# A hybrid decoder trunk on one Trainium2 core: adaLN dot products over 2048 columns at once, in two buffers of 2048 columns instead of three of 1024

## The chip, the cores and the metric

One core of one Trainium2 chip runs the whole program. The metric is the device time of one execution in microseconds (us); lower is better. The median of three runs of the kernel before is 2453.43 us (2445.65 to 2476.61).

## What is computed

Two layers of a decoder on 256 tokens of width 2048, all in float32. Each layer begins from a modulation that depends on one conditioning vector `c`; what follows is a token mixer with four head groups and a feed-forward network (FFN) with a short convolution:

```python
cond = silu(c)                                   # (1, 2048)
for l in range(2):
    mod = cond @ ada_w[l] + ada_b[l]             # ada_w[l]: 2048 x 12288
    sh1, sc1, g1, sh2, sc2, g2 = split(mod, 6)   # six vectors of 2048
    h = rms_norm(x, norm_mix[l]) * (1 + sc1) + sh1
    x = x + g1 * hybrid_mixer(h, ...)
    h = rms_norm(x, norm_ffn[l]) * (1 + sc2) + sh2
    x = x + g2 * conv_glu_ffn(h, ...)
```

The matrix `ada_w` is 100 MB a layer, a third of all that is read from HBM for both layers. Only the product of one row vector with it is needed.

## The kernel before

**Layout and stages.** Activations stand transposed: 128 channels on the partitions, the 256 tokens on the free axis, 16 channel chunks. Weights come from HBM in chunks of 128 x 1024 (512 KB) into a ring of four buffers, `raw`. ScalarE (ACT) rounds a chunk to `hi` (line 247), VectorE (DVE) subtracts to get `lo` (line 249), and TensorE (PE) multiplies with both (lines 279, 300, 304, 415). `hi` and `lo` have three buffers each. Stages run one after the other: layer 0's first stage (to about 160 us), its mixer (to 510), its FFN (to 1280), then the same for layer 1. In the FFN `up(g)` runs 22 times over 8 weight chunks each; the matrices of `down` follow in two parts, after g = 11 and after g = 21.

**The adaLN dots.** A product with `ada_w` is done on DVE, not on PE. There are 192 dots: 2 layers x 6 vectors (s = 0 to 5) x 16 channel chunks. A dot takes, for 128 output channels, 2048 columns of `ada_w`. They come in two halves of 128 x 1024, each with its own DMA (512 KB, `ada_load`, line 160) and its own multiply with `cond` that sums along the row (`ada_mul`, line 166, the `scalar_tensor_tensor` of line 167; its sum is fetched by a second small instruction, DVE_READ_ACCUMULATOR). The halves share a ring of three buffers of 1024 columns, the tag `adaw`. After four dots of a vector `ada_sum` (line 180) adds the two sums and the bias, for four chunks at once (lines 183 and 184).

**Who sets their order.** In layer 0's first stage (`mix_in_behind`, line 451) the dots of s = 1 and s = 0 for chunk k stand in line before the weight chunks of k: 32 dots, `ada_dot` at line 172. All others (160) are jobs of `ada_jobs` (line 187): `load_w` calls `tick`, which gives out jobs by a rate per weight chunk, and `mod` (line 225) forces those that are still missing when their vector is needed. A job loads its dot; its multiply is put behind the `lo` of that weight chunk. They get a low priority, and the scheduler that lays down the engines' queues places them among the rest. All DMAs are issued in order by the SP queue. A load of `adaw` waits there until its buffer's last multiply is done, and whatever stands behind it, the next weight chunk included, waits too. On DVE a multiply waits for its load, and the `lo` behind it waits too.

**Other places touched.** `nku` and `cT` (lines 821 and 967) are two small buffers of the sparse attention. `g` (line 1166) is the ring for the FFN's activations, 14 buffers, of which `down` needs 12 at once while one more is written. `Y_ORDER` and the names RATE, ADA_LATE, GATE are unchanged. An FFN begins with `norm_chunk` for 16 chunks (line 391), each with `t` (line 394), an ACT instruction (398) and an `act` (399); for the chunks c to c + 3 it needs the vectors s = 4 and s = 3 of these chunks.

## Time and profile before

| what | value |
|---|---|
| median of three runs | 2453.43 us |
| the profiled execution, its own time | 2452.41 us |
| its span (first to last instruction) | 2450.6 us |
| TensorE's mean granted clock | 0.987 of full |
| busy: PE / DVE / ACT | 2369.3 / 1937.6 / 1225.8 us |
| read from HBM | 603 MB, 248 GB/s over the span |

The profile is of one execution. A group of rows joins instructions of one line, engine and shape: its busy time, the mean of one, and the engine's idle time just before them with what ended it. Busy time of PE covers pipelined matmuls, so a busy PE is not yet one at its peak; how many matmuls it does in a stretch says more. The 1.8 us between span and time lie outside the first and last instruction.

### The profile page before, as it was taken

Reading aid. Unit: us, or ns where it says so; the run is one execution under the profiler, and the core shown is the slowest. Engines: PE = TensorE matmul, PEld = TensorE weight load, DVE = VectorE, ACT = ScalarE, POOL = GpSimd, SP = SyncE. Lnnn points to the kernel's source line nnn. Section 1 sums busy time; section 2 is a strip of 40 time slices with the busy share of each in tenths; the row PEclk is TensorE's granted clock in tenths of the full one; section 3 lists DMA queues with packets and bytes.
Section 4 is the critical chain, followed back from the end, with each engine's and each line's share of the span. In section 5 each row is a group of like instructions: output and inputs, shape, how many; then the busy total and the mean of one; then the engine's idle time right before and its main releaser. Section 6 shows DMA issues by size and latency. Waiting matters only on the chain.

```text
span 2450.6 us, 38162 instructions
## 1 busy us (share of the span) xinstructions
PE 2369.3 (97%) x14496; PEld 2100.5 (86%) x14496; DVE 1937.6 (79%) x3212; ACT 1225.8 (50%) x1880; POOL 25.2 (1%) x40
## 2 busy tenths in 40 slices
PE   7788999989999999999999999999999999999999
PEld 5666999978888888888879999998888888888887
DVE  6679988888888887888876999888887765566755
ACT  2124666446555534556335476554655553355543
POOL 0000000000000000000001000000000000000000
PEclk9999999999999999999999999999999999999999
DMA  9975787987777898778885567898667655556654
GB/s 326 328 275 183 246 270 270 336 290 255 256 255 248 297 320 293 260 240 270 288 295 168 187 218 244 269 321 317 236 231 241 224 191 191 189 186 196 190 190 164
DMA packets 169098, 609.82 MB, mean 249 GB/s; under 512 B 19025, under 2 KB 20945, under 8 KB 168401
## 3 DMA queue, kind: packets, MB, share of 16 engines
q1 hardware_dynamic: 168914, 607.39, 73.0%
q8 instruction: 113, 1.85, 0.3%
q14 instruction: 71, 0.58, 0.1%
HBM read 603.12 MB, written 4.19 MB: 248 GB/s over the span
## 4 chain that ended last, share of the span: by engine, by line
PE 84%; DMA 6%; DVE 6%; ACT 3%; issue 1%; SPq 0%; DVEq 0%; ACTq 0%
PE gt L300 39%; PE gt L304 20%; PE gt L279 9%; DMA adaw<-in_ada_dram 6%; PE gt L415 3%; PE pn L322 3%; DVE adaw L167 2%; PE po L591 1%; DVE lo L249 1%; PE pv L322 1%; PE pq L322 1%; PE s L565 1%; PE tp L586 1%; PE ss L382 1%; ACT hi L247 1%
## 5 line engine op out<-in xcount | busy, mean ns | idle before, releaser
L247 ACT CAST hi<-raw 128x1024 fp32r<-128x1024 f32 (+3 forms) x716 | 741.9, 1037 | 852.9 <-PE gt L300 602.2
L249 DVE TENSOR_TENSOR lo<-raw,hi 128x1024 fp32r<-128x1024 f32 (+3 forms) x716 | 859.7, 1204 | 358.0 <-ACT hi L247 356.3
L300 PE MATMUL gt<-act,hi 128*128 128x512 f32 x2816 | 983.7, 395 | 10.8 <-DVE act L399 7.8
L304 PE MATMUL gt<-act,lo 128*128 128x256 f32 x2816 | 786.6, 280 | 4.0 <-DVE lo L249 4.0
L300 PEld LDWEIGHTS gt<-act,hi 128*128 128x128 f32 x2816 | 530.9, 189 | 133.0 <-DVE act L399 8.6
L304 PEld LDWEIGHTS gt<-act,lo 128*128 128x128 f32 x2816 | 533.4, 190 | 5.3 <-DVE lo L249 5.3
L167 DVE SCALAR_TENSOR_TENSOR adaw<-adaw,cond 128x1024 f32<-128x1024 f32 x384 | 465.3, 1220 | 69.9 <-DMA adaw<-in_ada_dram 68.6
L300 PE MATMUL gt<-g,hi 128*128 128x512 f32 x1408 | 490.5, 394 | 0.2 <-DVE x L1179 0.2
L304 PE MATMUL gt<-g,lo 128*128 128x256 f32 x1408 | 393.0, 279 | 0.0
L300 PEld LDWEIGHTS gt<-g,hi 128*128 128x128 f32 x1408 | 264.4, 188 | 60.3 <-issue 0.4
L279 PE MATMUL gt<-act,hi 128*128 128x256 f32 x1600 | 303.2, 287 | 0.0
L304 PEld LDWEIGHTS gt<-g,lo 128*128 128x128 f32 x1408 | 265.7, 189 | 0.3
L279 PEld LDWEIGHTS gt<-act,hi 128*128 128x128 f32 x1600 | 251.4, 191 | 1.4
L279 PE MATMUL gt<-act,lo 128*128 128x256 f32 x800 | 230.7, 288 | 1.5 <-DVE lo L249 1.5
L279 PEld LDWEIGHTS gt<-act,lo 128*128 128x128 f32 x800 | 153.1, 191 | 2.5 <-DVE lo L249 2.3
L415 PE MATMUL gt<-actw,raw 128*128 128x256 f32 x416 | 105.7, 417 | 26.7 <-ACT actw L396 26.7
L415 PEld LDWEIGHTS gt<-actw,raw 128*128 128x128 f32 x416 | 86.1, 210 | 46.1 <-ACT actw L396 32.6
L1155 ACT ACTIVATE u<-v,vec 128x256 f32<-128x256 f32 x176 | 96.7, 597 | 10.2 <-DVE v L1152 5.3
L621 DVE SCALAR_TENSOR_TENSOR acc<-ug,vec,acc 128x256 f32<-128x256 f32 x240 | 99.1, 478 | 0.0
L1156 DVE SCALAR_TENSOR_TENSOR u<-v,vec,u 128x255 f32<-128x255 f32 x176 | 80.1, 479 | 11.9 <-ACT u L1155 11.9
L1151 ACT COPY v<-gt 128x256 f32<-128x256 f32 x176 | 63.5, 369 | 47.5 <-PE gt L304 34.2
L1159 DVE SCALAR_TENSOR_TENSOR u<-v,vec,u 128x254 f32<-128x254 f32 x176 | 80.1, 479 | 2.6
(290 smaller groups left out, 2152.6 us busy)
## 6 DMA issues: line engine op xcount, KB each, us to landing
adaw<-in_ada_dram SPq DMA_DIRECT2D x384, 512.0 KB, 5.5
raw<-in_wup_dram SPq DMA_DIRECT2D x352, 512.0 KB, 4.3
raw<-in_wdn_dram SPq DMA_DIRECT2D x176, 512.0 KB, 4.4
raw<-in_wo_dram SPq DMA_DIRECT2D x64, 512.0 KB, 5.2
raw<-in_wconv_dram SPq DMA_DIRECT2D x32, 512.0 KB, 4.3
raw<-in_wsqk_dram SPq DMA_DIRECT2D x32, 512.0 KB, 4.3
raw<-in_wlq_dram SPq DMA_DIRECT2D x32, 448.0 KB, 4.8
raw<-in_wnkv_dram SPq DMA_DIRECT2D x32, 412.0 KB, 3.4
```

Source lines behind the costliest of these rows:

```text
L167: nc.vector.scalar_tensor_tensor(w, w, 1.0, cond[:, hf * 1024:hf * 1024 + 1024], op0=ALU.mult, op1=ALU.mult, accum_out=raw[:, hf, j:j + 1],)
L247: nc.scalar.copy(hi[:, :n], raw[:, :n])
L249: sub = nc.vector.tensor_sub(lo[:, :n], raw[:, :n], hi[:, :n].bitcast(F32))
L279: nc.tensor.matmul(ps[m // 2][:, m % 2, :], ww[:, c], x, start=(k == 0 and i == 0 and m % 2 == 0), stop=(k == K - 1 and i == len(prods) - ...
L300: nc.tensor.matmul(banks[m].rearrange("p a t -> p (a t)"), hi[:, c], x2, start=(k == 0), stop=False, skip_group_check=True,)
L304: nc.tensor.matmul(banks[m][:, 1, :], lo[:, c], acts[k][:, 0, :], start=False, stop=(k == K - 1), skip_group_check=True,)
L322: nc.tensor.matmul(o, x[:, tt * P:(tt + 1) * P], ww[:, kk * N + c0:kk * N + c1], start=(k == 0 and i == 0 and first), stop=(k == K - 1 and ...
L415: nc.tensor.matmul(ps[m // 2][:, m % 2, :], ww[:, m * P:(m + 1) * P], xx, start=(first and i == 0 and m % 2 == 0), stop=(last and i == len ...
L621: nc.vector.scalar_tensor_tensor(acc[:, c, :], ug[:, c, j:j + T], w, acc[:, c, :], op0=ALU.mult, op1=ALU.add)
L1155: nc.scalar.activation(u[:, q, :], v, AF.Identity, scale=w2, bias=fb[:, i:i + 1])
L1156: nc.vector.scalar_tensor_tensor(u[:, q, 1:], v[:, :T - 1], w1, u[:, q, 1:], op0=ALU.mult, op1=ALU.add)
L1159: nc.vector.scalar_tensor_tensor(u[:, q, 2:], v[:, :T - 2], w0, u[:, q, 2:], op0=ALU.mult, op1=ALU.add)
```

## The change

The buffer of a dot now holds all 2048 columns, there are two of them, and its two DMAs of 512 KB are issued one after the other into its halves. The 160 dots of `ada_jobs` are one multiply over 2048 columns with one sum; `ada_sum` becomes one addition. The 32 dots of layer 0's first stage keep two multiplies of 1024 columns. To make room, `nku` and `cT` move into the ring `nsq` and `g` has 13 buffers.

```diff
-    def ada_load(l, s, j, hf):
-        w = ap_.tile([P, D // 2], F32, tag="adaw", name="adaw", bufs=3)
+    def ada_load(l, s, j):
+        w = ap_.tile([P, D], F32, tag="adaw", name="adaw", bufs=2)
         with tc.issue_after(last_load[0].ins) if gate[0] else ExitStack():
-            nc.sync.dma_start(w, io["ada"][l, s * KD + j, hf])
+            for hf in range(2):
+                nc.sync.dma_start(w[:, hf * 1024:hf * 1024 + 1024], io["ada"][l, s * KD + j, hf])
         return w
-    def ada_mul(w, s, j, hf, raw):
-        nc.vector.scalar_tensor_tensor(
-            w, w, 1.0, cond[:, hf * 1024:hf * 1024 + 1024], op0=ALU.mult, op1=ALU.mult,
-            accum_out=raw[:, hf, j:j + 1],
-        )
+    def ada_mul(w, out, c):
+        nc.vector.scalar_tensor_tensor(w[:, c], w[:, c], 1.0, cond[:, c], op0=ALU.mult, op1=ALU.mult, accum_out=out)
     def ada_dot(l, s, j, raw):
+        w = ada_load(l, s, j)
         for hf in range(2):
-            ada_mul(ada_load(l, s, j, hf), s, j, hf, raw)
+            ada_mul(w, raw[:, hf, j:j + 1], slice(hf * 1024, hf * 1024 + 1024))
...
-        nc.vector.tensor_add(m[:, c], raw[:, 0, c], raw[:, 1, c])
-        nc.vector.tensor_add(m[:, c], m[:, c], vec(l, "ada_b")[:, s * KD + j - 3:s * KD + j + 1])
+        nc.vector.tensor_add(mods[l, s][:, c], raw[:, c], vec(l, "ada_b")[:, s * KD + j - 3:s * KD + j + 1])
...
-                        for hf in range(2):
-                            dots.append(partial(ada_mul, ada_load(l, s, j, hf), s, j, hf, raw[s]))
+                        dots.append(partial(ada_mul, ada_load(l, s, j), raw[s][:, j:j + 1], slice(0, D)))
...
-            u = mp.tile([P, 3, 2, 64], F32, tag="nku", name="nku", bufs=1)
+            u = mp.tile([P, 512], F32, tag="nsq", name="nku")[:, 0:384].rearrange("p (b g d) -> p b g d", b=3, g=2)
...
-            cT = mp.tile([P, T], F32, tag="cT", name="cT", bufs=1)
+            cT = mp.tile([P, 2, T], F32, tag="nsq", name="cT")[:, 0, :]
...
-                y_ = fp.tile([P, 2, 2, T], F32R, tag="g", name="g", bufs=14)
+                y_ = fp.tile([P, 2, 2, T], F32R, tag="g", name="g", bufs=13)
```

SP's queue in layer 0's first stage, before; each `adaw` is one half, and a wait that names DVE is the one for a free buffer:

```order
L163 DMA adaw_244<-in_ada_dram 128x1024 [waits DMAHW2_49,DVE_49]
L163 DMA adaw_247<-in_ada_dram 128x1024 [waits DMAHW3_49,DVE_49]
L242 DMA raw_251<-in_wconv_dram 128x1024 [waits DMAHW4_49,PE_49]
L163 DMA adaw_253<-in_ada_dram 128x1024 [waits DMAHW5_49,DVE_49]
L163 DMA adaw_256<-in_ada_dram 128x1024 [waits DMAHW6_49,DVE_49]
L242 DMA raw_274<-in_wlq_dram 128x896 [waits DMAHW7_49,PE_49]
```

The same place after, where two DMAs fill one buffer:

```order
L164 DMA adaw_240<-in_ada_dram 128x1024 [waits DMAHW2_49,DVE_49]
L164 DMA adaw_240<-in_ada_dram 128x1024 [waits DMAHW3_49]
L239 DMA raw_246<-in_wconv_dram 128x1024 [waits DMAHW4_49,PE_49]
L164 DMA adaw_248<-in_ada_dram 128x1024 [waits DMAHW5_49,DVE_49]
L164 DMA adaw_248<-in_ada_dram 128x1024 [waits DMAHW6_49]
L239 DMA raw_268<-in_wlq_dram 128x896 [waits DMAHW7_49,PE_49]
```

Nothing changes place there; the second half of a dot no longer waits for a multiply of its own: before it waited for the first half of the dot just ahead, now the pair waits together for the dot two ahead.

DVE's queue at the beginning of layer 0's FFN, before; `modr0_4` and `modr0_3` receive the sums of the halves of the last dots that the FFN's norm needs, `t1` and `act` belong to `norm_chunk`:

```order
L167 SCALAR_TENSOR_TENSOR adaw_4657,modr0_4_2227<-adaw_4657,cond_85 128x1024
L399 SCALAR_TENSOR_TENSOR act_4603<-t1_4649,mod0_3_2230,act_4603 128x256
L399 SCALAR_TENSOR_TENSOR act_4603<-t1_4653,mod0_3_2230,act_4603 128x256
L249 TENSOR_TENSOR lo_4820<-raw_4816,hi_4818 128x1024
L249 TENSOR_TENSOR lo_4842<-raw_4838,hi_4840 128x1024
L167 SCALAR_TENSOR_TENSOR adaw_4468,modr0_3_2228<-adaw_4468,cond_85 128x1024
L167 SCALAR_TENSOR_TENSOR adaw_4659,modr0_4_2227<-adaw_4659,cond_85 128x1024
L167 SCALAR_TENSOR_TENSOR adaw_4470,modr0_3_2228<-adaw_4470,cond_85 128x1024
L249 TENSOR_TENSOR lo_4864<-raw_4860,hi_4862 128x1024
L249 TENSOR_TENSOR lo_4928<-raw_4918,hi_4926 128x1024
L167 SCALAR_TENSOR_TENSOR adaw_4663,modr0_3_2228<-adaw_4663,cond_85 128x1024
```

And after, from the last dot but one to the fourth `lo` of the FFN:

```order
L168 SCALAR_TENSOR_TENSOR adaw_4535,modr0_4_2159<-adaw_4535,cond_85 128x2048
L396 SCALAR_TENSOR_TENSOR act_4471<-t1_4502,mod0_3_2162,act_4471 128x256
L396 SCALAR_TENSOR_TENSOR act_4471<-t1_4506,mod0_3_2162,act_4471 128x256
L391 SCALAR_TENSOR_TENSOR t1_4511<-x_3377,amul_4467,actw_4456 128x256
L391 SCALAR_TENSOR_TENSOR t1_4515<-x_3377,amul_4467,actw_4456 128x256
L182 TENSOR_TENSOR mod0_4_2161<-modr0_4_2159,vs0_140 128x4
L168 SCALAR_TENSOR_TENSOR adaw_4541,modr0_3_2160<-adaw_4541,cond_85 128x2048
L396 SCALAR_TENSOR_TENSOR act_4472<-t1_4511,mod0_3_2162,act_4472 128x256
L396 SCALAR_TENSOR_TENSOR act_4472<-t1_4515,mod0_3_2162,act_4472 128x256
L391 SCALAR_TENSOR_TENSOR t1_4519<-x_3377,amul_4467,actw_4456 128x256
L391 SCALAR_TENSOR_TENSOR t1_4523<-x_3377,amul_4467,actw_4456 128x256
L246 TENSOR_TENSOR lo_4636<-raw_4632,hi_4634 128x1024
```

(Between the last two rows stand two instructions of 128 x 4: `amul` and the sum of s = 3.) Before, 14 halves (7 dots) stand behind the last addition to `x` of the mixer, and 9 `lo` of the FFN stand among them; now 5 dots stand there, all ahead of the FFN's fourth `lo` (counted from 1), and the last three of them are loaded in a row on SP.

## Rows read from the trace of the kernel before

**Rows 1.** The page, engines over the span: busy us (share) xinstructions.
```profile
PE 2369.3 (97%) x14496; PEld 2100.5 (86%) x14496; DVE 1937.6 (79%) x3212; ACT 1225.8 (50%) x1880; POOL 25.2 (1%) x40
```
**Rows 2.** Busy time by stretch: us, each engine's busy time (instructions), PEclk, DMA share, GB/s.
```profile
0.00:160.00 160.00, 123.20 (x470) 97.81 (x471) 105.64 (x220) 25.90 (x46) 0.40 (x5) 0.94 0.93 330
...
250.00:500.00 250.00, 247.77 (x1959) 236.43 (x1959) 217.24 (x399) 144.03 (x281) 4.21 (x6) 1.00 0.82 285
...
520.00:560.00 40.00, 33.02 (x155) 26.81 (x155) 33.98 (x63) 13.78 (x21) 0.00 (x0) 0.86 0.81 278
...
700.00:750.00 50.00, 50.00 (x290) 44.06 (x289) 41.15 (x62) 27.83 (x39) 0.00 (x0) 1.00 0.74 247
...
1172.00:1188.00 16.00, 11.55 (x63) 9.88 (x62) 12.95 (x26) 5.47 (x6) 0.00 (x0) 0.95 0.85 304
...
1400.00:1650.00 250.00, 245.52 (x1859) 230.49 (x1858) 224.30 (x439) 155.87 (x331) 5.68 (x9) 1.00 0.75 257
```
**Rows 3.** The chain that ended last, 40 to 60 us: start, us, what.
```profile
39.43 5.46 DMA adaw<-in_ada_dram
...
49.01 5.48 DMA adaw<-in_ada_dram
```
**Rows 4.** As rows 2: 13 chunks of the first stage, and its fullest 10 us.
```profile
29.33:150.59 121.26, 98.51 (x399) 81.20 (x398) 82.49 (x170) 11.86 (x26) 0.00 (x0) 0.92 0.95 332
...
100.00:110.00 10.00, 8.45 (x40) 7.12 (x39) 7.23 (x15) 0.91 (x2) 0.00 (x0) 1.00 0.97 366
```
**Rows 5.** Groups of instructions by shape: busy us, mean ns of one | idle before.
```profile
L249 DVE TENSOR_TENSOR lo<-raw,hi 128x1024 fp32r<-128x1024 f32 x672 | 819.9, 1222 | 353.9 <-ACT hi L247 352.3
...
L339 DVE TENSOR_TENSOR g<-u,g 128x512 fp32r<-128x512 f32 x44 | 30.1, 684 | 0.0
```
**Rows 6.** Timeline of DVE: start us, us, what, in two places.
```profile
43.64 1.23 DVE L167 SCALAR_TENSOR_TENSOR adaw<-adaw,cond 128x1024 f32<-128x1024 f32 x1 [0.33 <-DMA adaw<-in_ada_dram]
...
44.92 1.23 DVE L167 SCALAR_TENSOR_TENSOR adaw<-adaw,cond 128x1024 f32<-128x1024 f32 x1
...
1170.15 1.22 DVE L167 SCALAR_TENSOR_TENSOR adaw<-adaw,cond 128x1024 f32<-128x1024 f32 x1
...
1171.30 1.22 DVE L167 SCALAR_TENSOR_TENSOR adaw<-adaw,cond 128x1024 f32<-128x1024 f32 x1
...
1173.77 0.16 DVE L184 TENSOR_TENSOR mod<-mod,vs 128x4 f32<-128x4 f32 x1
```
**Rows 7.** DVE's `adaw` by stretch: us, its busy time (rows), clock, DMA.
```profile
250.00:500.00 250.00, 91.37 (x150) 1.00 0.82 285
...
1400.00:1650.00 250.00, 78.07 (x128) 1.00 0.75 257
```
**Rows 8.** Timeline at the start of layer 0's FFN, DVE, PE and SP.
```profile
508.23 3.23 DVE L1117 SCALAR_TENSOR_TENSOR x<-gt,mod,x 128x256 f32<-128x256 f32 x8 [0.18 <-PE gt L279]
...
516.08 0.88 DVE L394 SCALAR_TENSOR_TENSOR t<-x,amul,actw 128x256 f32<-128x256 f32 x2 [1.20 <-ACT actw L344]
...
518.54 0.79 PE L300 MATMUL gt<-act,hi 128*128 128x512 f32 x1 [3.46 <-DVE act L399]
...
536.18 9.92 SPq L163 DMA_DIRECT2D adaw<-in_ada_dram  x6
...
541.97 1.23 DVE L167 SCALAR_TENSOR_TENSOR adaw<-adaw,cond 128x1024 f32<-128x1024 f32 x1 [1.25 <-DMA adaw<-in_ada_dram]
...
554.13 0.74 PE L304 MATMUL gt<-act,lo 128*128 128x256 f32 x4 [2.83 <-DVE lo L249]
```
**Rows 9.** Timeline at the second part of layer 0's `down`.
```profile
1177.51 1.23 DVE L167 SCALAR_TENSOR_TENSOR adaw<-adaw,cond 128x1024 f32<-128x1024 f32 x1 [1.76 <-DMA adaw<-in_ada_dram]
...
1186.28 1.04 PE L382 MATMUL ss<-sq,ones 128*128 128x256 f32 x2 [4.45 <-DVE sq L380]
```
**Rows 10.** Waits over the span, then in 0:160: us in total, times, longest.
```profile
DVE adaw L167 <- DMA adaw<-in_ada_dram: 68.6, 84, 2.6
...
DVE adaw L167 <- DMA adaw<-in_ada_dram: 25.5, 36, 1.9
```

More of the change, by code (lines that the diff above doesn't have):

```diff
@@ L181, in ada_sum @@
         c = slice(j - 3, j + 1)
-        m = mods[l, s]
-        nc.vector.tensor_add(m[:, c], raw[:, 0, c], raw[:, 1, c])
-        nc.vector.tensor_add(m[:, c], m[:, c], vec(l, "ada_b")[:, s * KD + j - 3:s * KD + j + 1])
+        nc.vector.tensor_add(mods[l, s][:, c], raw[:, c], vec(l, "ada_b")[:, s * KD + j - 3:s * KD + j + 1])
         ready.add((l, s, j))
@@ L189, in ada_jobs @@
             for ss in ((2,), (4, 3), (5,)) if l == 0 else ((1, 0), (2,), (4, 3), (5,)):
-                raw = {s: cp.tile([P, 2, KD], F32, name=f"modr{l}_{s}") for s in ss}
+                raw = {s: cp.tile([P, KD], F32, name=f"modr{l}_{s}") for s in ss}
                 for s in ss:
```

## The prediction

> **What bounds the kernel now.** I read the page's engine shares first: PE is busy for 97% of the span, DVE for 79% [rows 1]. Busy PE time hides waiting, so the next view was the busy time by stretch with the count of matmuls. In the middle of an FFN PE starts 290 matmuls in 50 us, 5.8 a us, and is never idle [rows 2]: there PE is the bound, and whatever DVE saves is hidden. That holds for some 1750 of the 2450 us. Elsewhere there are five places where something else ends last.
>
> First, layer 0's first stage (0 to 160 us): PE is idle for 37 of 160 us, the DMA engines are busy for 93% [rows 2]. The chain of waits shows the loop: a load of `adaw` lands, its half is multiplied, a buffer comes free, the next load starts and lands 5.5 us later; a turn from one chunk to the next takes 49.01 - 39.43 = 9.6 us [rows 3]. Second and third, the two mixers: PE is idle for only 2.2 and 4.5 of 250 us, but DVE is 87 and 90% busy [rows 2] and is often what comes last. Fourth, the start of layer 0's FFN: from 520 to 560 us PE starts 155 matmuls where 5.8 a us would be 232, so 77 / 5.8 = 13.3 us are lost [rows 2]. The timeline says why: SP takes 9.9 us over six half loads, because each waits for a buffer; DVE waits for such a load; PE waits 2.83 us for a `lo` that stands behind it [rows 8]. Fifth, the second part of `down`: 63 matmuls in 16 us instead of 93, 5.2 us lost; DVE waits 1.76 us for `adaw`, and PE a little later 4.45 us [rows 2, 9].
>
> **The instructions.** 160 dots lose one multiply and one read of the sum each, 40 `ada_sum` lose one addition. The duration over 2048 columns stands nowhere in the trace. From `g` with 512 columns (684 ns) to `lo` with 1024 (1222 ns) a column costs 538 / 512 = 1.05 ns [rows 5]. Back to back a half occupies DVE from 1170.15 to 1171.30, 1.15 us; so a whole dot occupies 1.15 + 1.08 = 2.23 us instead of 2.30 and saves 0.07. Where a half must first wait for its own load the distance is 1.28 us (43.64 to 44.92) [rows 6], and the whole saves 0.07 + 2 x 0.13 - 0.13 = 0.20. So 160 dots give 11 to 32 us of DVE, the additions 40 x 0.16 = 6 us [rows 6]. At the low end a whole dot could cost as much as two halves, a saving of 0; at the high end the whole first halves' read and start (1.28 - 1.08 = 0.20) go; I take 0.13.
>
> **First stage.** Instructions stay as they are; the ring is now four halves deep. SP's queue has the same order, but the second half of a dot and the weight chunk behind it no longer wait for the first half of the dot ahead, so they are issued one half earlier, 1.3 us or more. A chunk k moves 4 x 0.524 + 0.524 + 0.459 = 3.08 MB (four halves, `wconv`, `wlq`), at 332 GB/s 9.3 us, which is what the loop shows: DMA is nearly full already, at 0.95 [rows 4]. If it were full all the time, at 332 / 0.95 = 349 GB/s, the turn would be 8.8 us, 0.45 us less. 14 turns gain 6 us. Bounds: the fullest 10 us moved 366 GB/s [rows 4], that is 8.4 us a turn and 12 us in all; on the other side, pairs issued together could delay a weight chunk that PE waits for, by one half's transfer (1.5 us) in one turn of five: +4. I take -6.
>
> The Trainium skill (DMA: Bandwidth & Descriptors, section "Where 436 GB/s comes from") gives about 358 GB/s as a core's share of HBM. By it the turn would be 8.6 us and the gain 10 us, in place of 6; this trace has 10 us at 366 [rows 4], so the page's figure is at least no wall for a single core.
>
> **Mixers.** 250 to 500 holds 150 rows of `adaw`, two per half: 37 dots; 1400 to 1650 holds 128, 32 dots [rows 7]. At 0.13 a dot and 0.16 for each of 9 and 8 additions DVE saves 6.3 and 5.4 us. I put 40% of that on PE's path, since PE is idle so little: -2.5 and -2. Against it, the scheduler lays out the mixer anew, with dots up to 9 weight chunks earlier, and a dot is now one block of 2.2 us in front of a softmax step. Bounds for both together: -12 (all of it reaches PE), +8 (one dot in nine of the 69 holds up PE by the 1.08 us that it is longer).
>
> **FFN start of layer 0.** After the order of the changed kernel, two `lo` run, then five dots stand among the norm's steps, and the fourth `lo` only behind the last dot. I follow DVE from the last addition to `x` (508.23 + 3.23 = 511.5 [rows 8]). Two `lo` end at 513.9, the first dot at 516.2. The first `t` can start at 516.1, as now [rows 8]; two `t`, then the second dot to 519.3: the first `act` comes 1.2 us later than now. The third dot's load has waited for the first dot's buffer (516.2) and needs some 6 us for two halves (5.5 for one in a full queue [rows 3]); DVE gets there at 522.8, about when it lands. The fourth ends near 529, the fifth, loaded after 525.1, near 533.3, the fourth `lo` near 536.5. PE starts 1.2 us after the 518.54 of now [rows 8] and has three weight chunks, 3 x 16 / 5.8 = 8.3 us, with some 3 us more because it runs at 1.2 GHz for a while after a wait (a mean of 0.86 of 2.4 GHz over 40 us is 11 us at the lower level [rows 2]). It runs dry at 531 and loses 5.5 us, then 2 to 3 us at the lower clock, plus the 1.2: 9 us instead of 13. I take -4. Bounds: -13 if the loads are early enough, +4 if each of the last three lands 5 us late and half of that reaches PE, less the 4.
>
> **Second part of `down`.** Loads of a pair are issued with one wait, and one dot stands where three halves stood; DVE's 1.76 us should go, and with it most of PE's 5.2, since its wait began there. I take -3; bounds -5 and +2 (one whole dot, 2.2 us, in front of the additions to `x`).
>
> **Everything else is nothing.** In the FFNs PE covers it (idle 0 of 50 us [rows 2]); if that cover were gone, the 60 or so dots there would give -4 to -12. 13 buffers for `g` hold the 12 that `down` reads and the one written; the next `g` comes behind `down` on PE anyway. `nku` and `cT` in the ring `nsq` wait for readers that stand ahead of them on DVE already; if not, one or two 0.7 us steps a layer, within the mixers' bounds. Layer 1's first stage has no dots in line.
>
> **Sum.** -6 - 4.5 - 4 - 3 = -17.5. The profiled execution took 2452.4 us (span 2450.6 and 1.8 around it), 1 us under the median of 2453.4. So 2435 us.
>
> **Rivals.**
> *A, slower: a dot at the head of DVE waits for both halves.* Now a first half is multiplied while the second is still landing; as one instruction the whole 2.2 us begins when the later half has landed. DVE waited 68.6 us in 84 waits for `adaw`, 36 of them in the first stage [rows 10], whose dots keep their halves: 48 others. If each became 1.15 us longer and half reached PE, as `hi` and `lo` have only three buffers, that is 48 x 1.15 / 2 = +28, less the first stage's 6: 2475 us. It decides where loads are still late; against it, every load may now start earlier than before. The Trainium skill (Perfetto Trace Analysis, section "Optimizing Scalar/DVE Operations") says that where Vector is not saturated but causes bubbles elsewhere, breaking instructions up can help; this change does the opposite, and by that rule A, 2475, would be the result. The 2.83 us wait of PE behind a dot [rows 8] is such a bubble; but there both halves were late, so the trace bears the rule out only in part.
> *B, nothing: the deeper ring finds DMA full at 0.95, the stalls only move.* The gains left are 2 or 3 us: 2451. For it: the FFN start still has five dots in a row and a loop through two buffers.
> *C, all of it:* the first stage runs at 366 GB/s (-12), the FFN start loses almost nothing (-11), `down` -5, the mixers -9: 2416.
>
> **How the numbers follow.** The forecast 0.45, B 0.25, A 0.15, C 0.15. The forecast's own spread is 2425 to 2445. For 8 in 10 I go to 2414 (most of C) and to 2463 (B whole, the milder part of A). Two per cent, 49 us, is about what a measurement of this kernel can tell from no change (its runs differ by 31 us): under 2404 needs more than C, 0.04; over 2502 needs twice A, 0.03; within, 0.93.
>
> **What would show it.** Right: a 2048-column multiply near 2.29 us, 160 of them; the first stage's turn near 8.9 us and DMA at 0.98 or more there; DVE's waits for `adaw` under 50 us; PE's loss from 520 to 560 smaller but not gone, at one place, ahead of the fourth `lo`; no 4 us wait of PE at the second `down`. Wrong: waits for `adaw` that are fewer but longer (A), a first stage of the same length (B), or a PE wait of over 8 us at the FFN's start.

## Result and profile after

The changed kernel takes 2469.6 us (median of 22 runs, 2464.3 to 2484.3), the kernel before 2459.6 us in the same series (22 runs, 2443.5 to 2483.5). The ratio is 1.0059, 95% interval 1.0037 to 1.0082: slower by 9 to 20 us. The forecast was 2435, with a range of 2414 to 2463. The profiled execution of the changed kernel took 2476.8 us, its span is 2475.0 (before 2452.4 and 2450.6).

What the change promised of the instructions is there. The page's engines, over the span of the changed kernel (before: [rows 1]):
```profile
PE 2380.4 (96%) x14496; PEld 2100.9 (85%) x14496; DVE 1918.3 (78%) x2852; ACT 1224.9 (49%) x1880; POOL 25.8 (1%) x40
```
360 instructions of DVE are gone and 19.3 us of its busy time. PE has 11 us more, with the same number of matmuls.

Busy time by stretch, the changed kernel, the stretches of [rows 2] and the 121 us of [rows 4]. Columns: stretch, us, busy us and instructions of PE, PEld, DVE, ACT, POOL, granted clock, DMA share, GB/s:
```profile
0.00:160.00 160.00, 127.30 (x518) 100.28 (x519) 113.49 (x235) 34.31 (x62) 6.48 (x13) 1.00 0.92 346
250.00:500.00 250.00, 240.56 (x1871) 227.75 (x1870) 208.63 (x305) 137.17 (x266) 3.37 (x5) 0.99 0.80 282
520.00:560.00 40.00, 31.70 (x155) 27.21 (x156) 35.32 (x59) 18.89 (x32) 0.00 (x0) 0.87 0.58 208
700.00:750.00 50.00, 50.00 (x285) 43.41 (x284) 42.25 (x56) 28.27 (x40) 0.00 (x0) 1.00 0.75 249
1172.00:1188.00 16.00, 16.00 (x92) 13.84 (x91) 15.51 (x19) 9.38 (x11) 0.00 (x0) 1.00 0.89 313
1400.00:1650.00 250.00, 240.61 (x1759) 225.16 (x1758) 219.34 (x374) 150.82 (x325) 5.80 (x9) 0.99 0.71 243
...
29.33:150.59 121.26, 100.93 (x453) 84.73 (x452) 87.87 (x183) 16.86 (x36) 0.00 (x0) 1.00 0.97 366
```
The first stage is quicker: 518 matmuls in 160 us where there were 470, and DMA at 0.97 and 366 GB/s where it was 0.95 and 332. Both mixers are slower: 1871 for 1959 and 1759 for 1859 matmuls in 250 us, with PE idle for 9.4 us where it was 2.2 and 4.5. The middle of the FFN has 285 instead of 290 matmuls, at a busy share of 1 and a clock of 1.00 in both; this is told of at the end.

Fixed windows slide against the work when a stage gets longer, so from here on stages are cut by the work: by the `lo` of DVE, one for each weight chunk and in the same order in both kernels (716). "Layer 0's mixer" runs from the 1st `lo` to the 97th (it takes in the start of the FFN), "layer 1's mixer" from the 385th to the 469th. The windows of these `lo` (stretch, us, busy us of `lo` and their number, clock, DMA share, GB/s), the kernel before:
```profile
209.22:602.09 392.87, 112.36 (x96) 0.97 0.80 275
...
1413.05:1752.72 339.67, 99.41 (x84) 0.99 0.78 270
```
and the changed kernel:
```profile
196.30:603.22 406.92, 112.00 (x96) 0.96 0.76 265
...
1424.96:1777.17 352.21, 99.13 (x84) 0.98 0.74 259
```
The first `lo` comes 12.9 us earlier; the first mixer takes 14 us longer, so that at its end all of it is lost again; the second takes another 12.5 us.

One execution scatters, so the two kernels were profiled three more times each. Times in us, each the distance between two such rows; the FFNs are the 204 chunks behind the 97th and the 240 behind the 469th:

| kernel, execution | first `lo` | layer 0's mixer | layer 0's FFN | 301st to 385th | layer 1's mixer | layer 1's FFN | span |
|---|---|---|---|---|---|---|---|
| before, 1 | 209.2 | 392.9 | 564.6 | 246.3 | 339.7 | 667.1 | 2450.6 |
| before, 2 | 210.1 | 390.9 | 564.6 | 245.6 | 340.2 | 679.8 | 2462.6 |
| before, 3 | 207.4 | 393.1 | 575.3 | 245.9 | 341.2 | 667.1 | 2460.8 |
| before, 4 | 214.3 | 390.9 | 564.6 | 244.1 | 343.1 | 679.8 | 2468.2 |
| changed, 1 | 196.3 | 406.9 | 578.1 | 243.6 | 352.2 | 667.1 | 2475.0 |
| changed, 2 | 196.7 | 405.4 | 574.9 | 243.8 | 344.7 | 667.1 | 2463.4 |
| changed, 3 | 195.1 | 406.7 | 571.5 | 243.8 | 345.6 | 667.1 | 2460.5 |
| changed, 4 | 195.6 | 402.8 | 573.4 | 245.5 | 345.1 | 667.1 | 2460.3 |

By the means: first stage -14.3, layer 0's mixer +13.5, layer 0's FFN +7.2, second part of `down` with layer 1's first stage (301st to 385th) -1.3, layer 1's mixer +5.9, layer 1's FFN -6.4, rest -0.3, together +4.3. Outside the FFNs it is +3.5: the mixers give back 19.4 us and with that more than the first stage gains. The mean of four spans carries the FFNs' scatter of 10 to 13 us each; that the full series has +14.5 (by its ratio) and the four +4 is left open below.

PE's clock has a part in it. From the 1st to the 97th `lo` the granted clock is 0.97 to 0.98 in the four executions of the kernel before and 0.95 to 0.96 in those of the changed one. Unrounded, the means are 0.975 and 0.959. With levels of 1.2 and 2.4 GHz that is 20 and 33 us at the lower one; at half the clock the 13 to 14 us more cost up to 7, by this estimate, of the 13.5 us. In layer 1's mixer the clock is 0.99 before and 0.98 to 0.99 in the changed kernel.

Where the first stage gains: the chain that ended last, the changed kernel (start, us, what; before: [rows 3]):
```profile
36.17 6.57 DMA adaw<-in_ada_dram
...
44.40 6.19 DMA adaw<-in_ada_dram
...
52.26 6.73 DMA adaw<-in_ada_dram
```
A turn takes (52.26 - 36.17) / 2 = 8.0 us at this place where it was 9.6: a load takes longer to land, but it is issued earlier. DVE's waits for `adaw` in the changed kernel (in total, times, longest), over the span and in 0 to 160 us, against 68.6 in 84 and 25.5 in 36 of [rows 10]:
```profile
DVE adaw L168 <- DMA adaw<-in_ada_dram: 75.8, 67, 3.2
...
DVE adaw L168 <- DMA adaw<-in_ada_dram: 12.0, 22, 2.0
```
The first stage's half goes away, the rest of the program has 63.8 us in 45 waits instead of 43.1 in 48. In layer 0's mixer (250 to 515 us) the group of the multiplies, first the kernel before, then the changed one (busy us, mean ns | idle before, releaser):
```profile
L167 DVE SCALAR_TENSOR_TENSOR adaw<-adaw,cond 128x1024 f32<-128x1024 f32 x81 | 98.0, 1219 | 11.3 <-DMA adaw<-in_ada_dram 11.1
```
```profile
L168 DVE SCALAR_TENSOR_TENSOR adaw<-adaw,cond 128x2048 f32<-128x2048 f32 x39 | 89.2, 2287 | 26.1 <-DMA adaw<-in_ada_dram 24.9 <-issue 1.1
```
A whole dot lasts 2.287 us, as forecast, but DVE idles 15 us more in front of them. One such place, the end of layer 0's mixer and the start of its FFN in the changed kernel (start, us, engine, what, idle before and its releaser; before: [rows 8]):
```profile
509.59 2.29 DVE L168 SCALAR_TENSOR_TENSOR adaw<-adaw,cond 128x2048 f32<-128x2048 f32 x1 [3.20 <-DMA adaw<-in_ada_dram]
...
511.81 3.22 DVE L1114 SCALAR_TENSOR_TENSOR x<-gt,mod,x 128x256 f32<-128x256 f32 x8
512.71 0.63 ACT L373 ACTIVATE sq<-x 128x512 f32<-128x512 f32 x1 [4.70 <-DVE x L1114]
513.39 1.26 PE L379 MATMUL ss<-sq,ones 128*128 128x256 f32 x4 [3.47 <-ACT sq L373]
...
523.62 0.50 PE L297 MATMUL gt<-act,hi 128*128 128x512 f32 x1 [4.54 <-DVE act L396]
...
539.41 1.22 PE L301 MATMUL gt<-act,lo 128*128 128x256 f32 x4 [4.68 <-DVE lo L246]
```
A whole dot waits 3.20 us for its loads at the head of DVE's queue and then runs 2.2 us; behind it stand the additions to `x`, which PE's sums of squares need, and PE is idle for 3.47 us. At the second part of `down` the changed kernel has (before: [rows 9])
```profile
1186.49 2.29 DVE L168 SCALAR_TENSOR_TENSOR adaw<-adaw,cond 128x2048 f32<-128x2048 f32 x1 [0.49 <-DMA adaw<-in_ada_dram]
...
1199.88 0.75 PE L379 MATMUL ss<-sq,ones 128*128 128x256 f32 x2 [2.77 <-DVE sq L377]
```
a wait of 0.49 us for 1.76, and of PE 2.77 for 4.45.

### The profile page after: what moved, and what is told of

The parts are those of the page before. It is cut to its first block, busy times and chain, and to the rows that moved or that the text cites. A ratio compares the mean times of both kernels' runs of the same rounds, so it can differ in the third digit from the quotient of the medians.

```text
span 2475.0 us, 37845 instructions
## 1 busy us (share of the span) xinstructions
PE 2380.4 (96%) x14496; PEld 2100.9 (85%) x14496; DVE 1918.3 (78%) x2852; ACT 1224.9 (49%) x1880; POOL 25.8 (1%) x40
## 4 chain that ended last, share of the span: by engine, by line
PE 79%; DMA 9%; DVE 7%; issue 2%; ACT 2%; SPq 0%; DVEq 0%; ACTq 0%
PE gt L297 39%; PE gt L301 20%; DMA adaw<-in_ada_dram 8%; PE gt L276 6%; PE pn L319 3%; PE gt L412 3%; DVE adaw L168 2%; DVE lo L246 2%; PE pv L319 1%; PE po L588 1%; PE s L562 1%; PE pq L319 1%; DMA raw<-in_wo_dram 1%; DVE acc L618 1%; ACT hi L244 1%
## 5 line engine op out<-in xcount | busy, mean ns | idle before, releaser
L168 DVE SCALAR_TENSOR_TENSOR adaw<-adaw,cond 128x2048 f32<-128x2048 f32 (+1 forms) x224 | 443.1, 1982 | 77.9 <-DMA adaw<-in_ada_dram 75.8
L412 PE MATMUL gt<-actw,raw 128*128 128x256 f32 x416 | 96.1, 389 | 22.4 <-ACT actw L393 22.4
L412 PEld LDWEIGHTS gt<-actw,raw 128*128 128x128 f32 x416 | 79.5, 194 | 39.0 <-ACT actw L393 28.3
L1148 ACT COPY v<-gt 128x256 f32<-128x256 f32 x176 | 63.8, 370 | 56.2 <-PE gt L301 35.9
```

Of the source, the lines that this page charges most:

```text
L168: nc.vector.scalar_tensor_tensor(w[:, c], w[:, c], 1.0, cond[:, c], op0=ALU.mult, op1=ALU.mult, accum_out=out)
L412: nc.tensor.matmul(ps[m // 2][:, m % 2, :], ww[:, m * P:(m + 1) * P], xx, start=(first and i == 0 and m % 2 == 0), stop=(last and i == len ...
```

## Experiments

Ratios are against the kernel before, timed beside each, with 95% intervals. Stage times are of the profiled execution, cut as above. Theory 1 was that a whole dot costs because it must wait for both halves; theory 2, that the room edits and the order that they lead to cost; theory 3, that buffers which come free in pairs cost. Lines of the diffs are cut to the core.

**again.** No edit.

> The changed kernel once more, unaltered, for a second profiled execution. In the first one the FFN of layer 0 took 2.83 us from one weight chunk's lo to the next (570 to 1170 us, 204 chunks) where the kernel before took 2.77; over the stage that is 14 of the 24 us by which the two profiled spans differ. If this pace belongs to the kernel, it is 2.83 again and the span is again near 2475. If it belongs to the execution (as the times of the changed kernel suggest, which lie at 2464 to 2470 or at 2476 to 2484 with nothing between), a span near 2464 goes with 2.77 and one near 2477 with 2.83. The two mixers should lose 11 and 13 us in either case. Ratio 1.006.

Measured: 1.0047 (1.0016 to 1.0078); span 2463.4, the second row of the changed kernel in the table. The mixers lost 12.5 and 5 us against the first execution of before. Layer 0's FFN again ran at the slower pace, layer 1's at the quicker. So the mixers' loss belongs to the kernel, though in layer 1 its size scatters.

**room.**
```diff
-u = mp.tile([P, 3, 2, 64], F32, tag="nku", name="nku", bufs=1)
+u = mp.tile([P, 512], F32, tag="nsq", name="nku")[:, 0:384].rearrange(...)
-cT = mp.tile([P, T], F32, tag="cT", name="cT", bufs=1)
+cT = mp.tile([P, 2, T], F32, tag="nsq", name="cT")[:, 0, :]
-... tag="g", name="g", bufs=14)
+... tag="g", name="g", bufs=13)
```


> The kernel before with nothing but the three edits that make room: nku and cT in the ring nsq, 13 buffers for g. The dots stay two halves, in three buffers of 1024. Theory 1 (a whole dot at the head of DVE waits for both of its halves, some 12 us in each mixer): no change, ratio 0.998 to 1.002, DVE's waits for adaw in the mixers 11 and 10 us as before. Theory 2 (the shared ring and the order that the scheduler then lays out cost the mixers 11 and 13 us): ratio 1.005 to 1.010, both mixers longer by 10 us or more. Theory 3 (buffers that come free only in pairs): no change, as theory 1.

Measured: 1.0064 (1.0029 to 1.0098); mixers 397.7 and 346.6 us (before 391 to 393 and 340 to 343). Theory 2 holds in part: without any whole dot the edits that make room cost 5 us a mixer. That is one execution, and ring4 below, with the same three edits, does not have the loss. The one wait on the shared ring in that trace is 0.7 us long; the rest would be the order, which the scheduler lays out anew, but that was not tried apart.

**ring4.**
```diff
 (with the three edits of room)
-w = ap_.tile([P, D // 2], F32, tag="adaw", name="adaw", bufs=3)
+w = ap_.tile([P, D // 2], F32, tag="adaw", name="adaw", bufs=4)
```


> The room edits, and four buffers of 1024 in place of three; the dots stay two halves with a load and a buffer each. Theory 1: the first stage gains what the changed kernel gained there (10 to 20 us at its end) and the mixers lose nothing, DVE's waits for adaw there under 11 us each: ratio 0.991 to 0.996. Theory 2: the mixers lose 24 us as in the changed kernel, the first stage gains 12: ratio 1.004 to 1.007. Theory 3: as theory 1, 0.991 to 0.996.

Measured: 0.9869 (0.9827 to 0.9912), 2430.0 us. The same memory as the changed kernel's two buffers of 2048, but four separate halves: the first `lo` comes at 186.5 us, 10 us ahead of the changed kernel. The windows of its mixers' `lo`:
```profile
186.49:577.86 391.37, 112.69 (x96) 0.97 0.80 276
...
1387.65:1724.84 337.19, 99.29 (x84) 0.99 0.77 270
```
and of its first stage, with engines as above, and DVE's waits for `adaw` in 0 to 160 us:
```profile
29.33:150.59 121.26, 110.16 (x479) 89.59 (x478) 95.51 (x199) 21.60 (x45) 6.17 (x8) 1.00 0.97 376
```
```profile
DVE adaw L167 <- DMA adaw<-in_ada_dram: 2.3, 4, 0.7
```
The first stage's waits are all but gone (25.5 before, 12.0 in the changed kernel), and the mixers lose nothing. Since a pair's buffer is filled again only when its second multiply is done, theory 3 holds for the first stage: of 23 us that a fourth half brings there, pairs get 13.

**split2.**
```diff
-dots.append(partial(ada_mul, ada_load(l, s, j), raw[s][:, j:j + 1], slice(0, D)))
+w = ada_load(l, s, j)
+for hf in range(2):
+    dots.append(partial(ada_mul, w, raw[s][:, hf, j:j + 1], slice(hf * 1024, hf * 1024 + 1024)))
```


> The changed kernel with each dot in line taken as two multiplies of 1024, each of which needs only its own half load, into the two sums of before; two buffers of 2048 and the pair of loads stay. Theory 1: the second half's transfer is hidden by the first half's multiply again, DVE's waits for adaw in the two mixers fall from 25 and 23 us to 12 to 15, and both mixers come back to within 4 us of the kernel before: ratio 0.993 to 0.998. Theory 2 (the order and the shared ring): as the changed kernel, 1.004 to 1.008. Theory 3 (a buffer of two halves comes free, and is filled again, only when the second multiply is done): the waits stay above 20 us in each mixer, ratio 1.003 to 1.008.

Measured: 0.9997 (0.9962 to 1.0032). The windows of its mixers' `lo`:
```profile
196.70:591.53 394.83, 112.38 (x96) 0.97 0.78 274
...
1410.80:1750.89 340.09, 99.26 (x84) 0.99 0.77 269
```
With the loads, the buffers and the room edits of the change, but two multiplies for one, layer 1's mixer is back, and layer 0's to within 3 us of the mean of before (8 us in mixhalf below, which has the same order on DVE there). With the ratio this shows that the long instruction makes most of the loss, not the pairs. Yet DVE's waits for `adaw` in the mixers fell only from 24.9 and 23.4 to 17.4 and 14.1 us, so waiting is not the whole of it. The timeline of DVE shows another thing, split2 first:
```profile
297.35 1.22 DVE L168 SCALAR_TENSOR_TENSOR adaw<-adaw,cond 128x1024 f32<-128x1024 f32 x1
...
298.49 0.42 DVE L920 TENSOR_TENSOR nu<-nq,Sn 128x256 f32<-128x256 f32 x1
298.83 0.42 DVE L921 TENSOR_TENSOR nu<-nq,Sn 128x256 f32<-128x256 f32 x1
299.16 1.22 DVE L168 SCALAR_TENSOR_TENSOR adaw<-adaw,cond 128x1024 f32<-128x1024 f32 x1
```
and about the same place in the changed kernel:
```profile
296.32 2.29 DVE L168 SCALAR_TENSOR_TENSOR adaw<-adaw,cond 128x2048 f32<-128x2048 f32 x1 [0.55 <-DMA adaw<-in_ada_dram]
...
298.54 0.35 DVE L888 COPY kc<-pv 64x16 f32<-64x16 f32 x2
298.90 1.19 DVE L892 COPY vb<-pv 32x128 f32<-32x128 f32 x4
300.12 0.69 DVE L680 TENSOR_REDUCE scl<-nsq 128x8 f32<-128x512 f32 x1
...
300.84 1.22 DVE L627 TENSOR_TENSOR acc<-acc,mu 128x1024 f32<-128x1024 f32 x1
...
303.20 1.22 PE L632 MATMUL va<-sq,mean 128*128 128x256 f32 x2 [3.34 <-ACT sq L629]
```
Between the halves stand short steps of the softmax and of the norms; a whole dot has no such place, and they queue up behind it. PE then waits 3.34 us for what follows `acc`; that wait is not all the queue's, since `acc` also needs PE's `mu`, which ended only at 299.86, 1.0 us before `acc` began. In split2's order 261 instructions other than `lo` stand between the halves of the mixers' 85 dots, at 60 of them (dots whose first multiply stands between the 1st and the 73rd or the 385th and the 457th `lo`). That is theory 1b; waiting for both halves is 1a.

**swap, swap2.** In split2's loop, swap2 being the same kernel again:
```diff
-for hf in range(2):
+for hf in (1, 0):
```


> split2 with its two multiplies in the other order: the second half, whose load is issued last, is multiplied first, so that DVE's first step on a chunk waits for both halves as the whole dot does, while the steps stay 1.15 us long; every engine's order is that of split2. The mixers are measured from layer 0's first lo to its 73rd (before 308, the changed kernel 318 to 320, split2 310 us) and from the 385th to the 457th (306, 311 to 320, 307). Theory 1a (the whole dot costs because it waits for both halves): both mixers as in the changed kernel, 317 to 320 and 311 to 320, DVE's waits for adaw there 18 to 25 us each, ratio 1.003 to 1.007. Theory 1b (it costs because 2.3 us in one piece stand in front of the short steps that PE and ACT wait for): both mixers as in split2, 308 to 312 and 305 to 309, ratio 0.998 to 1.002.

> swap once more, for a second profiled execution. From the first lo to the 97th (layer 0's mixer and the start of its FFN) the kernel before took 391 to 393 us in four executions, the changed kernel 403 to 407, split2 395, swap 403, adjacent 392; from the 385th to the 469th (layer 1's) 340 to 343, 345 to 352, 340, 339 and 351. If waiting for both halves is what costs in layer 0 and not in layer 1: 401 to 405 and 338 to 342 again. If swap's 403 was a scatter of the execution: 393 to 397. Ratio 0.996 to 1.002 either way.

Measured: 0.9986 (0.9957 to 1.0015) and 0.9986 (0.9957 to 1.0016). Mixers of swap:
```profile
196.31:599.53 403.22, 112.59 (x96) 0.95 0.77 268
...
1420.48:1759.63 339.15, 99.37 (x84) 0.99 0.77 269
```
and of swap2 402.9 and 341.0 us. The first half's multiply now waits for the second's load. Layer 0's mixer takes 8 us more than in split2, twice, and layer 1's no more. But DVE's waits for `adaw` in layer 0's mixer only went from 17.4 to 18.9 and 20.6 us, and some 4 of the 8 us come in one place, from the 25th to the 29th `lo`. The windows of that place, columns as at the top, for split2, mixhalf (below), swap and swap2:
```profile
287.97:329.71 41.74, 37.85 (x280) 34.97 (x279) 39.07 (x86) 25.31 (x64) 0.31 (x1) 0.96 0.68 242
```
```profile
288.02:333.23 45.21, 41.10 (x278) 37.56 (x277) 39.14 (x86) 25.23 (x64) 0.32 (x1) 0.89 0.60 212
```
```profile
287.92:333.80 45.88, 41.98 (x278) 38.27 (x277) 39.21 (x85) 25.22 (x64) 0.31 (x1) 0.85 0.62 214
```
```profile
287.06:332.67 45.61, 41.33 (x280) 37.80 (x279) 39.24 (x86) 25.22 (x64) 0.31 (x1) 0.89 0.63 216
```
At 303 us PE waits 3.9 us for `qa`, in split2, mixhalf and swap alike; what differs is the granted clock of the stretch, 0.96 in split2 and 0.85 to 0.89 in the others. mixhalf does not swap: up to the 73rd `lo` it has split2's instructions on DVE in split2's order, and it takes 314.3 us to that `lo` where split2 takes 309.5 and swap and swap2 315.7 and 315.5. So the 8 us are not shown to come from waiting for both halves. 1 to 3 us in layer 0 are left for 1a, and nothing in layer 1; it stays open. The times do not show the 8 us either (0.3%, within their interval).

**adjacent, adjacent2.** Again on split2, adjacent2 being the same kernel again:
```diff
+half = nc.vector.scalar_tensor_tensor(w[:, :1024], ..., accum_out=raw[:, 0, j:j + 1])
+with tc.high_priority(offset=100000), tc.issue_after(half.ins):
+    ada_mul(w, raw[:, 1, j:j + 1], slice(1024, D))
```


> split2 with the second multiply of a dot put right behind the first on DVE: in split2 the scheduler has laid 215 short steps between the halves of the 64 dots of the two mixers (27 of 32 and 29 of 32 dots have some there), here 50 (13 and 7 dots). Loads, buffers and durations are those of split2. Theory 1b (the whole dot costs because the short steps that PE and ACT wait for can no longer stand between its halves): most of the changed kernel's loss comes back without a whole dot: mixers 315 to 320 us (split2 310, changed kernel 318 to 320) and 310 to 318 (307, 311 to 320), ratio 1.002 to 1.006. If the one long instruction itself costs, or something else that halves avoid wherever they stand: as split2, 0.998 to 1.001.

> adjacent once more, for a second profiled execution. If the missing places between the halves are what costs in layer 1 and not in layer 0: 390 to 394 us from the first lo to the 97th and 348 to 353 from the 385th to the 469th again. If the 351 was a scatter of the execution: 339 to 343 there. Ratio 0.998 to 1.004 either way.

Measured: 1.0014 (0.9979 to 1.0048) and 1.0002 (0.9972 to 1.0033). Mixers of adjacent:
```profile
196.77:588.48 391.71, 112.61 (x96) 0.98 0.79 275
...
1397.75:1748.32 350.57, 99.57 (x84) 0.98 0.75 260
```
and of adjacent2 396.2 and 347.2 us. Nothing is lost in layer 0 to the 97th `lo` (by the 73rd, as the first expectation has it, 315 and 319 us, given back at the FFN's start, 77 us for 85), and 7 to 10 us in layer 1, where the four executions with split2's order there (split2, swap, swap2, mixhalf) have 339 to 341. So 1b holds in layer 1's mixer; the times, which the first expectation put at 1.002 to 1.006 for it, do not show it. The changed kernel's loss against split2 is 10.6 us in layer 0 and 6.8 in layer 1 by the means. The second is of the size of adjacent's. The first is accounted for by neither run alone; whether the two kinds add up there, or the order that the scheduler lays out around whole dots costs by itself, was not tried.

**mixhalf.**
```diff
+if mixer[0]:
+    for hf in range(2):
+        dots.append(partial(ada_mul, w, raw[s][:, hf, j:j + 1], slice(hf * 1024, hf * 1024 + 1024)))
+else:
+    dots.append(partial(ada_mul, w, raw[s][:, 0, j:j + 1], slice(0, D)))
```
The flag is on for the chunks loaded up to the end of each mixer.

> The changed kernel with the dots that are loaded during the two mixers (and the stages ahead of them) taken as two multiplies, those loaded in the FFNs whole as in the change; the sums of the second half start at zero there. If the whole dot costs only in the mixers: as split2, ratio 0.997 to 1.002, mixers 308 to 312 and 305 to 309 us. If the whole dots in the FFNs cost too (at the FFN's start and the second part of down): 1.002 to 1.006, with the mixers back but the 73rd to the 97th lo longer than the 85 us of split2.

Measured: 0.9997 (0.9967 to 1.0027), as split2; mixers 399.8 and 339.0 us (split2 394.8 and 340.1). The 314.3 us to the 73rd `lo` lie above the 308 to 312 expected, by the place told of under swap. That two kernels with halves in the mixers both have 0.9997 says that the whole dots there cost the time, and that whole dots in the FFNs cost nothing that the times show.

**room_g.** Of room, only the 13 buffers for `g`.

> The kernel before with 13 buffers for g and nothing else; every engine's order is that of the kernel before. The prediction put this at nothing: ratio 0.998 to 1.002. If the 0.64% that the three room edits cost together come from g: 1.004 to 1.009 with the loss in the FFNs; if they come from nku and cT (mixers longer by 3 and 6 us in room): 0.998 to 1.002.

Measured: 1.0021 (0.9991 to 1.0051), mixers 390.5 and 341.8 us. So room's longer mixers come with `nku` and `cT`. The time itself cannot tell between nothing and half of room's loss.

**before2, before3, before4, after3, after4.** The two kernels again; their stages are in the table. The last four are one execution each.

> The kernel before, unaltered, for a second profiled execution: how far two executions of one kernel differ by stage. If the pace of the FFNs belongs to the execution, one or both of its FFNs may run at 2.82 us a weight chunk instead of 2.77 (10 to 13 us an FFN); the mixers should be within 4 us of 308 and 306, the first lo within 2 us of 209. Ratio 0.997 to 1.003.

> The changed kernel, third profiled execution. At equal pace of the FFNs its stages add up to 2453 and 2462 us in the first two, yet none of its 34 times lies under 2464, while 9 of the first 22 times of the kernel before lie under 2451, where its stages add up to 2450. If the changed kernel brings layer 0's FFN to the slower pace (575 us or more for 204 chunks instead of 565), it is there again; if the pace is drawn afresh in each execution, half of the next two should have 565.

> The changed kernel, fourth profiled execution; as for the third: 575 us or more in layer 0's FFN if the pace there belongs to the kernel, 565 in one of the two if it is drawn afresh.

> The kernel before, third profiled execution. The first two had 565 us in layer 0's FFN, and 667 and 680 in layer 1's. If the pace of layer 0's FFN belongs to the kernel, 565 again; if it is drawn afresh, 575 in one of the next two.

> The kernel before, fourth profiled execution; as for the third.

Measured for before2: 1.0002 (0.9969 to 1.0036); before3, before4, after3 and after4 took 2462.6, 2470.1, 2462.2 and 2462.0 us. Layer 0's FFN took 564.6 us in three executions of before and 575.3 in one; in the changed kernel it began at the slower pace in all four, and in three it went over to the quicker one for a part. So the pace is drawn in part afresh, and that it leans to the slower side with the change is likely from four against four, and not shown. It need not be the dots: of all 20 profiled executions here, 13 of the 16 with 13 buffers for `g` have over 570 us, and one of the four with 14. room_g's interval of the time includes no difference, so this is open too.

**quarter.** On ring4, with the sums of the dots in a ring of four tiles:
```diff
+raw = {s: cp.tile([P, 4, KD], F32, tag="modr", name="modr", bufs=4) for s in ss}
+for i in range(2):
+    c = slice(i * 512, i * 512 + 512)
+    nc.vector.scalar_tensor_tensor(w[:, c], w[:, c], 1.0, cond[...], ..., accum_out=raw[:, 2 * hf + i, j:j + 1])
```


> ring4 with each half of a dot in line taken as two multiplies of 512 columns, so four pieces a dot; the first stage keeps its halves. By theory 1b the dose goes on: places for short steps between four pieces should shorten the mixers a little more (ring4: 307 and 305 us), 2 to 5 us each, against 2 x 0.13 us more of DVE in each of the 69 dots there, 9 us each in a stage where DVE is 87 to 90% busy. Both together: mixers 305 to 312 and 303 to 310, ratio 0.985 to 0.992 where ring4 had 0.987. If the pieces' overhead decides: 0.991 or more.

Measured: 0.9925 (0.9896 to 0.9955); mixers 306.1 and 303.3 us to the 73rd and the 457th `lo` (ring4: 307.0 and 304.8), but 91.6 us from the 73rd to the 97th (84.4). The loss at the FFN's start is not that of the pieces: ring4d, which has halves and the same ring of four tiles for the sums, has it too. Against ring4d quarters bring nothing, in the mixers or in the time: the gain from more places ends at halves.

**ring4d.** On ring4, `nku` in a buffer of its own, with room for it from the sums of the dots in a ring of four tiles, as in quarter.

> ring4 with nku in a buffer of its own again (the room comes from taking the sums of the dots from a ring of four tiles); cT stays in nsq, g has 13. If what room lost against room_g (its mixers 3 and 5 us longer) comes from nku's place in the ring: ratio 0.981 to 0.986, mixers 303 to 306 and 300 to 304 us. If it was only the order that the scheduler lays out, which differs here again, it could go either way by 4 us: 0.983 to 0.990.

Measured: 0.9925 (0.9892 to 0.9957); 305.0 and 304.5 us, and 91.4 at the FFN's start. It is no better than ring4, and outside both ranges expected; what the ring for the sums costs at the FFN's start was not tried alone.

**ring4_2.** ring4 again.

> ring4 once more, unaltered: the first interval rests on six runs, and its profiled execution had both FFNs at the quicker pace (2.77 us a weight chunk). If the gain is the kernel's, its first lo comes at 186 to 188 us (before 209) and its mixers take 304 to 310 and 302 to 308 us again, ratio 0.984 to 0.992. If the first result owed its size to the quicker pace alone, 0.992 to 0.997.

Measured: 0.9929 (0.9896 to 0.9963), first `lo` at 186.9 us, mixers 309.7 and 305.1 to the 73rd and the 457th. The gain is the kernel's, at the smaller end of the first interval: four separate halves beat the kernel before, by 9 to 42 us over the two intervals, and with it the changed one.

## Why the prediction was wrong

- **The base**: 2452.4 us, one execution, beside a median of three. The median of 22 is 2459.6, so 7 of the 35 us between 2435 and 2469.6 are not the change's.
- **The instructions**: right. 2.287 us for a forecast of 2.29, and the next step starts 298.54 - 296.32 = 2.22 us after it (2.23). The page's busy time of DVE fell by 19 us, within the 17 to 38 of the working.
- **First stage, -6**: right in kind, too small. -14.3 by the means of four, beyond the bound of -12. The turn went below the 8.8 us forecast (8.0 in the chain; 3.08 MB at 366 GB/s are 8.4): the value was taken at 349 GB/s, although [rows 4] showed 366 in ten of its own microseconds, and 366 is what the whole stage then ran at. The Trainium skill (DMA: Bandwidth & Descriptors, section "Where 436 GB/s comes from") has some 358 GB/s as a core's share; 366 and, in ring4, 376 GB/s over 121 us lie above it.
- **Mixers, -2.5 and -2, bounds -12 to +8 for both**: this is the step that failed. Measured +13.5 and +5.9 (to the 97th and the 469th `lo`). It credited 40% of 0.13 us a dot to PE, and had the block of 2.2 us in its bounds alone, at 1.08 us for one dot in nine. Cut in two again, in split2 and mixhalf, the same dots give 0.9997 for 1.0059 and 1.0047, and the mixers get back 14 to 17 of the 19.4 us. So the joined multiply costs where the working had it save. Of the ways in which it does, one is shown: a dot's halves were not one block cut in two, other steps stood between them (adjacent, layer 1). It could have been read beforehand: in the order of the kernel before, steps other than `lo` stand between the halves of 55 of the mixers' 84 dots. The other, the load of the second half landing under the first half's multiply, is rival A's; swap did not show it to cost. Nothing in the working allowed for PE's clock in the mixers, which by the estimate above is up to 7 us of layer 0's 13.5.
- **FFN start, -4**: the path was followed rightly, from a start that moved. The additions to `x` came 3.6 us later (511.81 for 508.23), behind the dot that waited 3.20 us. From there PE's first matmul came 11.8 us later (10.3 before; the working had 1.2 more), and PE's wait ahead of the fourth `lo` was 4.68 us (5.5). What was gained there was small: from the additions to the 97th `lo` 91.7 us by the mean of four, 92.2 before.
- **Second part of `down`, -3**: the waits shrank as forecast (0.49 and 2.77 us), but the stage gained 1.3 us.
- **`nku` and `cT` at nothing**: wrong by some 5 us a mixer in room, where the dots are as before, and not to be seen in ring4, which has the same edits and a fourth buffer; so not settled. The working had covered it by the mixers' bounds, which were too narrow.
- **Rival A** came nearest, and its sign came: waits for `adaw` that are fewer but longer, 67 with 75.8 us for 84 with 68.6. That its time, 2475, is so near the profiled execution's 2476.8 is luck in part. It had 48 waits each longer by 1.15 us; measured were 45 with 1.42 us each for 0.90 before, and the first stage gained 14 us where it had 6. That these waits are what costs is not shown (swap), and it did not have the missing places between the halves. The rule in the Trainium skill beside it (Perfetto Trace Analysis, section "Optimizing Scalar/DVE Operations": where Vector is not saturated but makes others wait, breaking instructions up may help) agrees with the runs: split2 has 0.9997 where the whole dots have 1.0059 and 1.0047. Down to 512 columns, in quarter, it gave nothing more.
- **Left open**: the stages outside the FFNs add up to +3.5 us, the times say +9 to +20. The FFNs' pace (below) could make up the rest, but in the four profiled executions of each kernel the two FFNs together differ by 1 us only. That 1 us is +7.2 in layer 0's and -6.4 in layer 1's, where the kernel before drew the slower pace twice and the changed one never. With equal draws there the stages would add up to 3.5 + 7.2 = 10.7 us, within the interval; that the draws were luck is likely and not shown.

## What to carry to other kernels

Before two instructions are joined into one on an in-order engine, look in the order at what stands between them: joined, they hold back all of it, and they start only when the later of their inputs is there; the 0.1 us that a joined dot saved on DVE did not pay for it here. In this kernel a ring was worth most in small buffers that come free one by one: the same 16 KB a partition gave 0.7 to 1.3% as four halves and nothing as two pairs (split2). An experiment's stage should be compared with more than one execution of its neighbour, and with the granted clock beside it: swap's 8 us looked like the cause until mixhalf had most of them without it. Where a stage was bound by loads, a gain there must be followed through the next stage before it is counted.

## What the runs showed of the hardware

PE has two paces in an FFN, at a granted clock of 1.00 and a busy share of 1 in both. The window from 700 to 750 us has 290 matmuls in the kernel before and 285 in the changed one [rows 2, and above], and layer 0's FFN takes 564.6 or 575.3 us, layer 1's 667.1 or 679.8, in kernels whose matmuls there are the same. The mean duration of one matmul of 512 columns from 570 to 1140 us shows it too, first the kernel before, then the changed one:
```profile
L300 PE MATMUL gt<-act,hi 128*128 128x512 f32 x1261 | 437.2, 391 | 0.0
```
```profile
L297 PE MATMUL gt<-act,hi 128*128 128x512 f32 x1222 | 431.3, 399 | 0.0
```
In the quicker pace a matmul of 512 columns and one of 256 together take 347 ns from start to start, in the slower one 353 on average, in a pattern that repeats after three such pairs. An FFN mostly keeps the pace with which it comes out of its start, for 600 us and more, and all four combinations of the two FFNs turned up. This is 11 and 13 us, as much as the effects studied here, and 23 of the 40 us by which runs of one kernel differ. What sets the pace was not found.
